# A one-layer streaming encoder step: spreading the last operand forms, a third sum of squares, an earlier root of x, and other loads in the head

## The chip, the cores and the metric

The kernel runs on one core of a Trainium2 chip. The metric is device time in microseconds of one execution. A core has a matrix engine (TensorE, "PE" in the profile, with its weight loads as "PEld"), VectorE ("DVE"), ScalarE ("ACT"), GpSimd ("POOL") and SyncE ("SP", which issues DMAs). Each engine works off its own queue in order; what is behind a waiting instruction waits too. A change is judged against the median of three runs of the kernel before.

## The reference, cut to what matters

Two groups of tokens, 512 of a prompt and 32 of a running stream, are put side by side as T = 544 columns. All is fp32.

```python
x  += concat(rmsnorm(short_conv(...)), rmsnorm(fox_attention(...))) @ w_out   # one input projection w_in for both
x  += cross_attention(rmsnorm(x), mk, mv, w_xq, w_xo)                         # 256 memory tokens, 4 heads
x  += square(relu(rmsnorm(x) @ w_up)) @ w_down                                # hidden 4 * 2048
y   = rmsnorm(x)                                                              # g_final
rmsnorm(x, g) = x * rsqrt(mean(x * x) + 1e-6) * g
logf = log_sigmoid(rmsnorm(x) @ w_f + b_f)                                    # 8 forget gates, part of w_in
```

D_MODEL is 2048, the hidden size of the MLP 8192. The outputs are y, the new keys, values and gates, and the last rows of the convolution.

## The kernel before, in words

Features lie on the 128 partitions and tokens on the free axis, so x is sixteen tiles of 128 x 544. Each fp32 operand is split in a high part that TensorE takes at its fast rate and the rest: `split(hi, lo, src)` is one ScalarE instruction (`hi`, line 84) and one VectorE instruction (`lo = src - hi`, line 85). A product then takes three matmuls: hi*hi, hi*lo, lo*hi. Weights come by DMA from SyncE as `raw` tiles and are split to `whi` and `wlo` in the same way, four buffers each.

The big projections work in a two-by-two block scheme with seven products: `operands` builds, from four 128 x 272 quarters of an input pair, the combinations `ts` and splits them (`oph`, `opl`); `combine` and `dsum` build the sums of weight blocks (`sum`). Weight sums and splits are given a priority 40 steps ahead of their place. The program is a list of operations that a scheduler puts in order for each engine, by its model of when each is ready; buffers of a pool with N slots are handed out again only when all reads of the former content, a DMA's included, are done.

The stages, in order of time, with the places that the change touches:

- **Head** (to about 60 us). Eight steps j load x tiles j and j+8 (`xr`) and one 128 x 1024 weight tile `w_first[j]`, scale x by the gain (`vec`), build the operands and run 48 matmuls into four PSUM pairs `heads`. The squares of x are summed: for j = 0 directly into two tiles `acc_x`, else by a square `sq` on ScalarE and a DMA on GpSimd's queue that adds it to `acc_x`. Behind the loop ScalarE copies the four pairs out (line 410), in the order 2, 3, 0, 1.
- **Gate product** `emit_logf` (line 430): 80 narrow matmuls with the weights of the forget gates, into a PSUM tile that is one of the two used by `heads`. The root of x, `rstd(acc_x)`, is called in `begin`, which is run in the first output pair of the input projection, between its third and fourth product; `begin` also scales the first four tiles by the root `rb` and runs the first convolution.
- Input projection, convolution, attention, output projection, cross-attention (to about 960 us).
- **Cross-attention's output** (about 915 to 976 us): `xo_done(m)` adds each output tile to x, squares it and scales it by the gain for the MLP; the squares go to two tiles `acc_3` by accumulating DMAs (line 1103). With the last tiles the first pair of MLP-up begins; `rstd(acc_3)` is called in that pair.
- **MLP-up** (to about 1650 us): 32 outputs. After each, `forms` writes seven combinations of the result as split operands to DRAM (`fd`). For the last two this is done in parts during MLP-down.
- **MLP-down** (1650 to 2333 us): eight column groups c with eight output pairs p each, 84 matmuls a pair. Products accumulate in PSUM tiles X, Y and Z; copies of intermediate states (`e1`, `e2`, lines 1350 to 1360) go out by ScalarE before X or Y is written again. For c = 0 and p = 1 to 6 one of six parts of `forms_in_parts` follows a pair; four of these hold four `put`s each. A `put` splits a 128 x 272 tile into `fp` (a tag with three buffers) and stores it by a DMA on GpSimd's queue. These forms are read in the last group, c = 7.
- **End** (2333 us on): the last output pair is done for the first half of the tokens (a = 0) and then the second (a = 1). `last_rstd` makes the root of each half, `finish` multiplies eight output pairs by it, `store` writes them. All eight of the first half are finished by VectorE, four behind each of the two outputs of a = 1; of the second half three are finished by GpSimd.

```python
        def put(dst, x):
            f = npool.tile([128, T], F32R, tag="rstd", name="fp", bufs=3)
            split(two(f)[:, 0], two(f)[:, 1], x)
            pool.dma_start(dst, f)
```

Of the kernel before, what the change touches and what calls it, by code (L numbers as in the profile page):

```python
# [41 lines left out]
def hybrid_step(  # L42
# [156 lines left out]
    def operands(x, b11, ts, tags):  # L199
        hi, lo = two(b11)[:, 0], two(b11)[:, 1]  # L200
        split(hi, lo, x[:, 0])
# [160 lines left out]
    for j in range(8):  # L362
        xr = [headp.tile([128, T], F32, tag="xr", name="xr", bufs=5) for i in range(2)]
        if j == 0:
            hi, lo = weights(w_first[j])
        for i in range(2):
            sp.dma_start(xr[i], xT[j + 8 * i])
        if j:
            hi, lo = weights(w_first[j])
        x = headp.tile([128, 4, TH], F32, tag="x", name="x", bufs=2)  # L370
        for i in range(2):
            if j + i == 0:
                dve.tensor_scalar(x[:, :2], two(xr[i]), gain(G_MIX, 0), None, ALU.mult)
            else:
# [13 lines left out]
        for i in range(2):  # L388
            if j:
                sq = tmp("sq")[:, :T]  # L390
                act.activation(sq, xr[i], AF.Square)
                pool.dma_start(acc_x[i], sq, accum_op=ALU.add)
            else:
                act.activation(acc_x[i], xr[i], AF.Square)
# [13 lines left out]
    for t, ps in ((2, heads[2]), (3, heads[3]), (0, heads[0]), (1, heads[1])):  # L408
        for a in range(2):
            act.activation(two(first_tiles[t])[:, a], ps[a], AF.Copy)  # L410
# [13 lines left out]
    def emit_logf():  # L424
        ps = mm_tile()
        plan = (("b11", 0), ("b21", 8)), (("b11", 0), ("t1", 0), ("b22", 8))
        for a in range(2):
            seq = [(j + k0, o[name][n]) for name, k0 in plan[a] for j, o in enumerate(xops) for n in range(2)]
            for i, (k, x) in enumerate(seq):
                pe.matmul(ps[:16, a, :TH], wf_hl[:, k], x, start=i == 0, stop=i == len(seq) - 1)  # L430
        return ps
# [144 lines left out]
    def begin():  # L576
        rstd(acc_x, D, out=rb)
# [515 lines left out]
    def xo_done(m, ps):  # L1093
# [4 lines left out]
        if j == 0:  # L1098
            act.activation(acc_3[i], x, AF.Square)
        else:  # L1100
            sq = (tmp("sq") if j > 4 else up.tile([128, 1024], F32, tag="raw2", name="sq", bufs=4))[:, :T]
            act.activation(sq, x, AF.Square)
            pool.dma_start(acc_3[i], sq, accum_op=ALU.add)
# [3 lines left out]
        if i:  # L1107
            b11 = upform.tile([128, T], F32R, tag="b11", name="b11")
            ops.append(operands(xgs.pop(j), b11, up.tile([128, 2 * T], F32, tag="sum", name="ts"), "ABC"))
# [68 lines left out]
    def forms_in_parts(i, h1, h2):  # L1178
# [15 lines left out]
        def first():  # L1194
            put(fd[i][0], a[:, 0])
            put(bd[i - NF + 4], a[:, 1])
            put(fd[i][5], b[:, 0])
            put(fd[i][3], b[:, 1])

        def second():  # L1200
            for t, q in zip(box["t"], ((1, 2), (4, 6))):
                for n in range(2):
                    put(fd[i][q[n]], t[:, n])

        return [differences, first, second]
# [123 lines left out]
    for c in range(NF // 4):  # L1329
# [8 lines left out]
        for p in range(8 if c < NF // 4 - 1 else 7):  # L1338
# [21 lines left out]
            act.activation(e2[:, 1], X, AF.Copy)  # L1360
# [8 lines left out]
            if c == 0 and 1 <= p <= len(parts):  # L1369
                parts[p - 1]()  # L1370
# [8 lines left out]
    sums = []  # L1379
    for a in range(2):  # L1380
        y = fin[a, 7] = slot("AB"[a], F32, "yout")
        sums.append([t[:, TH * a:TH * a + TH] for t in acc_4])
        for i in range(2):
# [13 lines left out]
            if a:  # L1397
                if i == 0:
                    rb_4 = last_rstd(sums[0])
# [3 lines left out]
    rb_5 = tmp("rb")[:, :TH]  # L1403
    act.activation(rb_5, rb_4, AF.Copy)
# [86 lines left out]
```

## Time and profile before

| what | value |
| --- | --- |
| median of 3 runs | 2365.38 us (2365.28 to 2366.73) |
| profiled execution, its own time | 2366.75 us |
| its span, first to last instruction | 2364.9 us |
| mean granted TensorE clock | 0.994 |
| instructions | 47573, of them 18083 matmuls |
| TensorE, VectorE, ScalarE, GpSimd busy | 98%, 85%, 56%, 10% |

In a row of a group of instructions stand line, engine, operation, the tile written and those read, the number, then busy time, the mean duration in ns, and the idle time of the engine just before them with what ended it. In a row of the timeline stand start, duration, engine, line, operation, tiles, shape, and in brackets the engine's idle time before it and the releaser. In a row of waits stand who waited for whom, then the total in us, the times and the longest. A line number can be that of a helper: 84 and 85 are all splits.

### The profile page before, as it was taken

The page shows a single profiled execution, that of the slowest core. Times are in us where ns is not written, and L with a number is a line of the kernel's source. Part 1 is how long each engine was busy: PE and PEld are TensorE (multiplying, and loading weights), DVE is VectorE, ACT ScalarE, POOL GpSimd, SP SyncE. Part 2 cuts the span into 40 slices and gives each one's busy share as a digit, 9 for nine tenths or more (in the row PEclk, how much of TensorE's full clock was granted, in tenths as well). Part 3 has the DMA queues.
Part 4 walks back from the last instruction along what each step waited for, and adds up shares of the span by engine and source line. Part 5 has one row for each costly group of instructions (what it writes and reads, how often), then busy time and mean ns, then how long its engine had stood idle before and what let it go on. Part 6 is the DMA issues. An engine that isn't in the chain of part 4 may idle for free. (4 is left out here: it accounts for less than half of the span.)

```text
span 2364.9 us, 47573 instructions
## 1 busy us (share of the span) xinstructions
PE 2310.9 (98%) x18083; PEld 2281.7 (96%) x18083; DVE 2008.1 (85%) x3562; ACT 1317.8 (56%) x2569; POOL 246.8 (10%) x447
## 2 busy tenths in 40 slices
PE   8999999999999999899999999999899999999997
PEld 8899999999999998899999999999799999999997
DVE  7899988877767757999999999998788888888885
ACT  8454555555644546665566656665455555555564
POOL 2000011113200001111111111111000000000001
PEclk9999999999999999999999999999999999999998
DMA  9333345578434537655666556668773564565454
GB/s 249 117 105 129 109 159 167 164 233 306 145 93 153 161 104 221 204 192 190 203 191 203 182 188 202 192 196 290 272 252 129 206 240 159 171 234 208 128 174 123
DMA packets 169638, 434.31 MB, mean 184 GB/s; under 512 B 19960, under 2 KB 24752, under 8 KB 169408
## 3 DMA queue, kind: packets, MB, share of 16 engines
q1 hardware_dynamic: 111616, 315.90, 39.8%
q0 software_dynamic: 52288, 106.45, 15.4%
q10 hardware_dynamic: 5504, 8.93, 1.1%
q8 instruction: 141, 2.31, 0.4%
q14 instruction: 89, 0.73, 0.1%
HBM read 322.27 MB, written 97.78 MB: 178 GB/s over the span
## 5 line engine op out<-in xcount | busy, mean ns | idle before, releaser
L84 ACT ACTIVATE whi<-raw 128x512 fp32r<-128x512 f32 x661 | 416.5, 631 | 466.8 <-PE mmx L269 95.4
L84 ACT ACTIVATE whi<-sum 128x512 fp32r<-128x512 f32 x676 | 422.4, 630 | 416.5 <-PE mmx L269 186.2
L85 DVE TENSOR_TENSOR wlo<-raw,whi 128x512 fp32r<-128x512 f32 x661 | 453.4, 688 | 123.5 <-ACT whi L84 115.8
L85 DVE TENSOR_TENSOR wlo<-sum,whi 128x512 fp32r<-128x512 f32 x676 | 453.1, 686 | 88.1 <-ACT whi L84 85.3
L1276 PE MATMUL dx<-f,whi 128*128 128x272 f32 x2016 | 389.6, 289 | 14.3 <-ACT e L1350 7.9
L269 PE MATMUL mmx<-oph,wlo 128*128 128x272 f32 x1296 | 374.9, 289 | 2.6 <-DVE wlo L85 2.6
L269 PE MATMUL mmx<-oph,whi 128*128 128x272 f32 x1296 | 373.5, 288 | 1.3 <-ACT h L278 0.9
L269 PE MATMUL mmx<-opl,whi 128*128 128x272 f32 x1296 | 372.1, 287 | 0.0
L1276 PEld LDWEIGHTS dx<-f,whi 128*128 128x128 f32 x2016 | 317.6, 189 | 16.5 <-ACT e L1350 9.7
L1276 PE MATMUL mm<-f,whi 128*128 128x272 f32 x1512 | 292.1, 288 | 0.0
L1276 PE MATMUL dx<-f,wlo 128*128 128x272 f32 x1008 | 291.3, 289 | 0.0
L269 PE MATMUL mmy<-oph,whi 128*128 128x272 f32 x864 | 249.8, 289 | 6.3 <-ACT whi L84 5.1
L269 PE MATMUL mmy<-oph,wlo 128*128 128x272 f32 x864 | 249.1, 289 | 0.9 <-DVE wlo L85 0.9
L269 PE MATMUL mmy<-opl,whi 128*128 128x272 f32 x864 | 248.8, 288 | 0.0
L269 PEld LDWEIGHTS mmx<-oph,wlo 128*128 128x128 f32 x1296 | 244.0, 188 | 3.2 <-DVE wlo L85 3.2
L269 PEld LDWEIGHTS mmx<-oph,whi 128*128 128x128 f32 x1296 | 244.7, 189 | 1.9 <-ACT h L278 1.1
L269 PEld LDWEIGHTS mmx<-opl,whi 128*128 128x128 f32 x1296 | 244.2, 188 | 0.0
L1276 PEld LDWEIGHTS mm<-f,whi 128*128 128x128 f32 x1512 | 238.2, 189 | 0.0
L1276 PE MATMUL mm<-f,wlo 128*128 128x272 f32 x756 | 218.1, 289 | 0.0
L1276 PEld LDWEIGHTS dx<-f,wlo 128*128 128x128 f32 x1008 | 190.6, 189 | 0.0
L269 PEld LDWEIGHTS mmy<-oph,whi 128*128 128x128 f32 x864 | 162.9, 189 | 7.5 <-ACT whi L84 5.5
L269 PE MATMUL mmx<-b,whi 128*128 128x272 f32 x864 | 167.8, 291 | 1.3 <-DVE x2r L1095 1.1
(412 smaller groups left out, 4941.5 us busy)
## 6 DMA issues: line engine op xcount, KB each, us to landing
raw<-in_w_up SPq DMA_DIRECT2D x128, 512.0 KB, 3.8
raw<-in_w_dn SPq DMA_DIRECT2D x128, 512.0 KB, 4.6
f<-fd SPq DMA_DIRECT2D x224, 272.0 KB, 5.7
fd<-form POOLq DMA_DIRECT2D x180, 272.0 KB, 4.0
raw<-in_w_in SPq DMA_DIRECT2D x88, 512.0 KB, 3.9
raw<-in_w_out SPq DMA_DIRECT2D x32, 512.0 KB, 3.9
acc<-sq POOLq DMA_DIRECT2D x40, 272.0 KB, 4.9
kq<-hl POOLq DMA_DIRECT2D x32, 256.0 KB, 3.1
```

What stands on the lines that cost most here:

```text
L84: act.activation(hi, src, AF.Copy)
L85: dve.tensor_tensor(lo, src, hi.bitcast(F32), ALU.subtract)
L269: pe.matmul(ps, a[:, c], x, start=first and j == 0 and n == 0, stop=j == 7 and n == 2, skip_group_check=not first)
L1276: pe.matmul(ps, a[:, c], f[:, x], start=first and j == 0 and n == 0, stop=j == 3 and n == 2, skip_group_check=not first)
```

## The change

- Head: x of step j+1 is loaded behind the weights of step j, and the squares of step j+1 are made at the end of step j. In the first step the order of the loads is x tile 0, half of the weights, x tile 8, the other half; the second x tile is scaled, and the second weight half split, behind the split of `b11` (which is taken out of `operands` and stands before each call of it).
- The PSUM pairs of the head are copied out in the order 0, 2, 3, 1, one half by ScalarE and one by VectorE.
- `rstd(acc_x)` is called inside the gate product, behind its first 32 matmuls.
- From the eleventh output tile on, the squares of cross-attention's output go to a third tile, the first directly and five by VectorE additions; the root then sums three tiles.
- `forms_in_parts` returns nine steps for each of the two outputs in place of three, and one step follows each output pair from the second on. What a step issues on ScalarE is ordered behind that pair's copy of X at line 1360 (`issue_after` is an order in ScalarE's queue, not a semaphore).
- The output y has the layout (half, pair, partition, 544), so that a store is one row a partition.
- Of the first half's eight outputs VectorE finishes two and GpSimd three when the root is there, and VectorE the last three behind the loop.

```diff
+    raws = [wpool.tile([128, 1024], F32, tag="raw", name="raw", bufs=3)[:, :512] for i in range(2)]
+    xn = load_x(0, lambda i: sp.dma_start(raws[i], w_first[0, :, 512 * i:512 * i + 512]))
     for j in range(8):
+        xr = xn
         if j:
             hi, lo = weights(w_first[j])
+        else:
+            hi, lo = halves(raws[0], 512)
+        if j < 7:
+            xn = load_x(j + 1)
...
+        split(two(b11)[:, 0], two(b11)[:, 1], x[:, 0])
+        if j == 0:
+            act.activation(x[:, 2:], two(xr[1]), AF.Identity, scale=gain(G_MIX, 8))
+            more = halves(raws[1], 512)
+            hi, lo = Parts([hi, more[0]]), Parts([lo, more[1]])
...
+        if j == 0:
+            square_x(0, xr)
+        if j < 7:
+            square_x(j + 1, xn)
...
-    for t, ps in ((2, heads[2]), (3, heads[3]), (0, heads[0]), (1, heads[1])):
-        for a in range(2):
-            act.activation(two(first_tiles[t])[:, a], ps[a], AF.Copy)
+    for t in (0, 2, 3, 1):
+        act.activation(two(first_tiles[t])[:, 0], heads[t][0], AF.Copy)
+        dve.tensor_copy(two(first_tiles[t])[:, 1], heads[t][1])
...
+            if a == 0:
+                rstd(acc_x, D, out=rb)
...
     def begin():
-        rstd(acc_x, D, out=rb)
...
+        elif i == 0 and j == 5:
+            acc_3.append(npool.tile([128, T], F32, tag="rstd", name="acc", bufs=3))
+            act.activation(acc_3[2], x, AF.Square)
         else:
...
-            pool.dma_start(acc_3[i], sq, accum_op=ALU.add)
+            if j < 5:
+                pool.dma_start(acc_3[i], sq, accum_op=ALU.add)
+            else:
+                dve.tensor_tensor(acc_3[2], acc_3[2], sq, ALU.add)
...
-        return [differences, first, second]
+        steps = [differences]
+        for dst, x in ((fd[i][0], a[:, 0]), (bd[i - NF + 4], a[:, 1]), (fd[i][5], b[:, 0]), (fd[i][3], b[:, 1])):
+            steps.append(lambda dst=dst, x=x: put(dst, x))
+        for n, q in enumerate(((1, 2), (4, 6))):
+            for k in range(2):
+                steps.append(lambda n=n, k=k, q=q: put(fd[i][q[k]], box["t"][n][:, k]))
+        return steps
...
-        d = slice(TH * a, TH * a + TH)
-        (sp if p % 2 else act).dma_start(o_y[2 * p:2 * p + 2, :, d].rearrange("m p t -> p m t"), two(y))
+        (sp if p % 2 else act).dma_start(o_y[a, p], y)
...
-            act.activation(e2[:, 1], X, AF.Copy)
+            mark = act.activation(e2[:, 1], X, AF.Copy)
...
-            if c == 0 and 1 <= p <= len(parts):
-                parts[p - 1]()
+            if parts and c + p:
+                with tc.issue_after(mark.ins):
+                    parts.pop(0)()
...
-                for p in range(4 * i, 4 * i + 4):
+            if a and i == 0:
+                rb_4 = last_rstd(sums[0])
+                rb_5 = pooled(rb_4)
+                for p in (0, 1):
                     store(p, 0, finish((0, p), rb_4, dve))
+                for p in (2, 3, 4):
+                    store(p, 0, finish((0, p), rb_5, pool))
+    for p in (5, 6, 7):
+        store(p, 0, finish((0, p), rb_4, dve))
```

More of the change, by code (lines that the diff above doesn't have):

```diff
@@ L361, in hybrid_step, with load_x, square_x @@
     xops = []
-    for j in range(8):
+    def load_x(j, between=lambda i: None):
         xr = [headp.tile([128, T], F32, tag="xr", name="xr", bufs=5) for i in range(2)]
-        if j == 0:
-            hi, lo = weights(w_first[j])
         for i in range(2):
             sp.dma_start(xr[i], xT[j + 8 * i])
+            between(i)
+        return xr
+    def square_x(j, xr):
+        for i in range(2):
+            if j:
+                sq = tmp("sq")[:, :T]
+                act.activation(sq, xr[i], AF.Square)
+                pool.dma_start(acc_x[i], sq, accum_op=ALU.add)
+            else:
+                act.activation(acc_x[i], xr[i], AF.Square)
+    raws = [wpool.tile([128, 1024], F32, tag="raw", name="raw", bufs=3)[:, :512] for i in range(2)]
+    xn = load_x(0, lambda i: sp.dma_start(raws[i], w_first[0, :, 512 * i:512 * i + 512]))
+    for j in range(8):
+        xr = xn
         if j:
             hi, lo = weights(w_first[j])
+        else:
+            hi, lo = halves(raws[0], 512)
+        if j < 7:
+            xn = load_x(j + 1)
         x = headp.tile([128, 4, TH], F32, tag="x", name="x", bufs=2)
[L371 to L374, printed above, removed]
+        if j == 0:
+            dve.tensor_scalar(x[:, :2], two(xr[0]), gain(G_MIX, 0), None, ALU.mult)
+        else:
+            for i in range(2):
                 act.activation(x[:, 2 * i:2 * i + 2], two(xr[i]), AF.Identity, scale=gain(G_MIX, j + 8 * i))
@@ L387, in hybrid_step @@
                                   stop=j + i == 8 and n == 2)
[L388 to L394, printed above, removed]
+        if j == 0:
+            square_x(0, xr)
+        if j < 7:
+            square_x(j + 1, xn)
     wf_hl = tpool.tile([128, T + 4], F32R, tag="t", name="wf_hl")[:, :256].rearrange("p (k c) -> p k c", k=KD)
@@ L1108, in xo_done @@
             b11 = upform.tile([128, T], F32R, tag="b11", name="b11")
+            split(two(b11)[:, 0], two(b11)[:, 1], xgs[j][:, 0])
             ops.append(operands(xgs.pop(j), b11, up.tile([128, 2 * T], F32, tag="sum", name="ts"), "ABC"))
@@ L1192, in differences @@
             dve.tensor_tensor(t34[:, 1], b[:, 0], t12[:, 1], ALU.subtract)
[L1194 to L1203, printed above, removed]
-        return [differences, first, second]
+        steps = [differences]
[5 more added lines that the diff above has]
+        return steps
     rb_3 = []
@@ L1379, in hybrid_step, with pooled @@
     sums = []
+    def pooled(r):
+        rp = npool.tile([128, T], F32, tag="rstd", name="rp", bufs=3)[:, :TH]
+        act.activation(rp, r, AF.Copy)
+        return rp
     for a in range(2):
@@ L1396, in hybrid_step @@
             act.activation(two(y)[:, i], xa, AF.Identity, scale=gain(G_FIN, 14 + i))
[L1397 to L1400 removed]
+            if a and i == 0:
+                rb_4 = last_rstd(sums[0])
+                rb_5 = pooled(rb_4)
+                for p in (0, 1):
                     store(p, 0, finish((0, p), rb_4, dve))
+                for p in (2, 3, 4):
+                    store(p, 0, finish((0, p), rb_5, pool))
+    for p in (5, 6, 7):
+        store(p, 0, finish((0, p), rb_4, dve))
     rb_4 = last_rstd(sums[1])
[L1403 to L1404 removed]
+    rb_5 = pooled(rb_4)
     for p in range(8):
```

6 lines of the change are left out of this document (3 added, 3 removed).

## The prediction

> **What bounds the kernel now.** I read the page first, then the busy time by stage, then what TensorE waited for, then for each long wait the instructions of the engine that ended it.
>
> ```profile
> span 2364.9 us, 47573 instructions
> PE 2310.9 (98%) x18083; PEld 2281.7 (96%) x18083; DVE 2008.1 (85%) x3562; ACT 1317.8 (56%) x2569; POOL 246.8 (10%) x447
> ```
> ```profile
> 8.24:60.50 52.26, 51.21 (x384) 50.90 (x384) 43.38 (x90) 46.14 (x91) 12.25 (x14) 1.00 0.96 252
> 60.50:102.00 41.50, 38.28 (x284) 35.15 (x284) 33.02 (x64) 16.04 (x31) 1.11 (x2) 0.96 0.28 93
> 102.00:900.00 798.00, 797.21 (x6180) 779.78 (x6180) 638.30 (x1228) 410.90 (x821) 84.00 (x157) 1.00 0.49 158
> 900.00:980.00 80.00, 71.17 (x519) 67.00 (x518) 64.55 (x112) 54.66 (x101) 13.19 (x16) 0.96 0.79 226
> 980.00:1650.00 670.00, 668.19 (x5323) 667.53 (x5322) 622.56 (x1016) 407.52 (x759) 112.74 (x214) 1.00 0.62 199
> 1650.00:1730.00 80.00, 66.50 (x498) 65.40 (x497) 62.90 (x119) 36.85 (x79) 7.43 (x14) 0.96 0.75 263
> 2352.40:2364.90 12.50, 0.00 (x0) 0.00 (x0) 4.49 (x9) 0.40 (x1) 3.92 (x3) 0.50 0.70 240
> ```
> The columns are TensorE, weight loads, VectorE, ScalarE, GpSimd, granted clock, DMA share, GB/s. TensorE carries the kernel: in 102 to 900 it is idle for 0.8 us of 798. An edit pays only where TensorE stands still or runs slowly, and those places are few:
>
> ```profile
> PE mm L386 <- ACT b L84: 8.2, 1, 8.2
> PE dx L1276 <- ACT e L1350: 7.9, 8, 3.3
> PE dx L1276 <- ACT e L1360: 6.4, 2, 4.4
> PE mmy L269 <- ACT whi L84: 5.1, 2, 3.1
> PE mmx L269 <- DVE wlo L85: 2.6, 2, 2.3
> ...
> PE mmx L269 <- DVE x2r L1095: 1.1, 1, 1.1
> PE mm L430 <- ACT hr L410: 1.1, 1, 1.1
> PE mmx L269 <- ACT h L278: 0.9, 1, 0.9
> ```
> The start, the two `dx` rows (all but 0.7 us of them at 1650 to 1730), the seam into MLP-up (5.1 and 1.1), the seam behind the head (2.3 of the 2.6, and 0.9), and the head's evacuation (1.1). Behind the long ones the clock was halved too:
>
> ```profile
> 8.24:14.24 6.00, 6.00 (x26) 5.90 (x27) 5.95 (x20) 5.95 (x12) 0.00 (x0) 1.00 0.94 338
> ...
> 92.75:96.17 3.42, 3.29 (x14) 3.29 (x15) 3.42 (x9) 1.93 (x3) 1.11 (x2) 0.50 0.31 78
> ...
> 963.15:969.98 6.83, 4.75 (x19) 4.43 (x20) 5.82 (x12) 5.41 (x10) 1.38 (x2) 0.50 1.01 305
> 1662.88:1666.30 3.42, 3.38 (x15) 3.38 (x16) 3.42 (x8) 2.06 (x4) 0.53 (x1) 0.50 1.05 416
> 1686.78:1690.19 3.41, 3.41 (x17) 3.41 (x16) 3.41 (x7) 0.98 (x3) 0.00 (x0) 0.50 0.05 20
> ```
> A busy half-clock stretch of 3.4 us costs 1.7 us. The first row shows 26 matmuls in 6 us (0.23 us each, against 498 in 66.5, 0.13): the start runs at half rate as well, though no clock was recorded yet.
>
> **Late forms (`forms_in_parts`), the main term.** Before, 16 `put`s stand in six parts in the first pairs of MLP-down. In 1650 to 1730 TensorE and, behind its wait, ScalarE wait:
>
> ```profile
> PE dx L1276 <- ACT e L1350: 7.1, 3, 3.3
> ```
> ```profile
> ACT fp L84 <- DMA fd<-fp: 19.4, 7, 6.0
> ...
> ACT fp L84 <- DMA bd<-fp: 2.7, 1, 2.7
> ```
> `fp` has three buffers, each free only when its store has landed; ScalarE's queue is in order, so a `put` that waits for its buffer holds back `whi` and the copies `e` out of PSUM, and TensorE waits for `e`. The edit makes 18 steps, one per output pair of some 10.5 us, each ScalarE part queued behind the pair's second `e2` copy. Three buffers then turn over in 31 us, so the 22.1 us of ScalarE waits should vanish, and with them 7.1 + 6.4 = 13.5 us of TensorE idle in this stretch and 2 x 1.7 of half clock: 16.9. What is late next is VectorE:
>
> ```profile
> 1730.00:1817.80 87.80, 87.80 (x703) 87.80 (x702) 78.05 (x136) 46.21 (x92) 0.00 (x0) 1.00 0.54 189
> ```
> 89% busy, 9.3 us of a 10.5 us pair. A `put` adds one 128x272 operation (0.43, row at 2349.10 below): 9.8, still room. The two `differences` steps add four: 11.1 us, 0.6 over in one pair each. Bounds of that: nothing, if the sums and weight halves prepared ahead absorb it, and 1.2. I charge 0.5. ScalarE (53% here) and GpSimd's queue hide the rest; the h tiles keep four of the seven `tmp` buffers for longer, and the three that are left serve `e1` and `e2`, two a pair. **Gain 16.4.**
>
> **Third sum of squares.**
> ```profile
> 960.15 0.66 ACT L1102 ACTIVATE sq<-x2r 128x544 f32<-128x544 f32 x1 [3.36 <-issue]
> ```
> ```profile
> 951.94 0.88 POOL L1103 DMA_DIRECT2D acc<-sq  x1 [3.14 <-DMA acc<-sq]
> ```
> ```profile
> DMA to landing us min/median/max: 3.6/5.6/8.1
> ```
> ```profile
> 961.48 0.73 DVE L205 TENSOR_TENSOR ts<-x 128x544 f32<-128x544 f32 x1 [3.13 <-ACT x L1106]
> ```
> ScalarE stands 3.36 us with no named releaser: 951.94 plus the longest landing, 8.1, is 960.0, so I read it as a square waiting for a `tmp` buffer that an accumulating DMA still reads. `x` queued behind it holds VectorE for 3.13, VectorE's sum holds `whi`, and TensorE idles 3.1. The edit takes six squares off the DMA chain and gives VectorE five 128x544 adds (0.65 each, from four in 2.62 below: 3.3). Three fall ahead of that sum, so the sum comes 3.1 - 2.0 = 1.1 earlier; the halved clock behind it (19 matmuls in 4.75, so 2.4 lost) probably goes, but VectorE sets the pace there and I take half: **gain 2.3**. Ends: -0.2 (adds fully exposed), and all 6.6 of idle plus 2.4, or 9.0. I stay near the low end because VectorE is the engine that TensorE waits for here. The two extra sum matmuls at the root cost about 0.5, in the same stretch and inside the bounds.
>
> **Head.** Before, the whole 512 KB weight is issued ahead of x, and on both engines the weight halves come ahead of x:
> ```profile
> 4.99 1.15 ACT L84 ACTIVATE whi<-raw 128x512 fp32r<-128x512 f32 x2 [2.53 <-DMA raw<-in_w_first]
> ```
> ```profile
> 6.87 0.50 DVE L373 TENSOR_SCALAR x<-xr,vec 128x544 f32<-128x544 f32 x1
> ```
> ```profile
> vec<-in_vecs ACTq DMA_DIRECT2D x1, 60.5 KB, 4.4
> ```
> The gains `vec`, issued at 0.74, land at 5.1; with x first, VectorE's multiply ends at 5.64 and two 128x272 splits on ScalarE (0.4 each) give a first matmul at 6.45 against 8.24: gain 1.8 (0 if the loads only swap places, 2.6 if the multiply alone remained). The half-rate stretch may shorten; by the 3.4 us and 6.8 us lengths above it is somewhere between 3.4 and 6.8 long against 6.0 now, worth -0.4 to 1.3, and I take the middle, 0.4. Moving each next x and its squares forward adds no instruction; it lets the accumulation chain end earlier. Evacuating the first PSUM pair first, half on VectorE (idle there, next row), removes the 1.1 wait. **Gain 3.3.**
>
> **Root inside the gate product.** VectorE's rows:
> ```profile
> 62.11 1.22 DVE L230 TENSOR_TENSOR sum<-raw,raw 128x1024 f32<-128x1024 f32 x1 [7.53 <-DMA raw<-in_w_in]
> ```
> ```profile
> 72.62 0.69 DVE L85 TENSOR_TENSOR wlo<-sum,whi 128x512 fp32r<-128x512 f32 x1 [4.55 <-ACT whi L84]
> ```
> It idles 4.55 us before 72.62, then is so loaded with the root and the first convolution that TensorE waits 2.3 at 90.6 and 0.9 at 101. The root's eight 128x272 operations (8 x 0.43 = 3.4) and what hangs on `rb` can start some ten us earlier and fill that hole. Its eight ssq matmuls are only moved. Gain 2.3 + 0.9 + 1.7 of clock = **4.9**; the low end is 1, if only the root moves and the convolution stays.
>
> [...]
>
> **Tail.**
> ```profile
> 2346.57 2.62 DVE L1293 TENSOR_TENSOR yout<-yout,r 128x544 f32<-128x544 f32 x4
> 2349.10 0.43 DVE L1392 TENSOR_TENSOR x<-x,mm 128x272 f32<-128x272 f32 x1
> 2349.45 2.61 DVE L1293 TENSOR_TENSOR yout<-yout,r 128x544 f32<-128x544 f32 x4
> ```
> The last add (L1392) stands behind four finished outputs, the last root behind four more. Two go instead of four ahead of it (1.3 saved), three instead of four ahead of the root (0.5): 1.8. The last stores run 6.8 us on full DMA engines:
> ```profile
> 2356.50:2363.30 6.80, 0.00 (x0) 0.00 (x0) 0.93 (x2) 0.00 (x0) 1.65 (x2) 0.50 0.96 329
> ```
> Each output's rows are twice as long in the new layout (2176 bytes in place of 1088). That saves nothing at worst, and 1.4 us if the 329 GB/s of this row become the 416 of the row at 1662.88; I take 0.8, a little over the middle, because the queues are full here. **Gain 2.6.**
>
> **Sum.** 16.4 + 2.3 + 3.3 + 4.9 + 2.6 = 29.5 us. The profiled execution took 2366.75, so 2337.25; the median of the three runs stands 1.4 lower, which gives 2335.9. I say 2336. About 0.2% (4.7 us) is what a measurement of this kernel can tell from no change.
>
> **Rivals.** *VectorE becomes the bound of the 18 pairs* (chance 0.18): 9.8 of 10.5 us leaves 0.7, and an in-order wait of VectorE for the delayed ScalarE half can eat it; at 0.5 us a pair 9 come back: 2345. *The edges do not spread the `put`s*, two fall together and the buffer waits remain (0.06): only 13.1 is gained, 2352. *Only the late forms work*, the seams stay because VectorE is short there (0.06): 2349.
> *Slower* (0.06): a `put`'s second half sits on VectorE's queue ahead of the next weight half and waits until ScalarE's copy behind the sixth product; then every pair stalls as the `e` L1350 waits did, 7.1 in three, 2.4 each, 18 x 2.4 = 43: 2379. It ends slower from 1.9 us a pair on. Against it: VectorE already waits for that copy in every pair (`xb += e2`) and those pairs show no gap. *No change* within 0.2% (0.02) needs several of these in part.
> A small one inside the forecast (0.1): three finished outputs on GpSimd, 1.32 us each, hold VectorE's root; two operations held gives 2.6 back, 2339.
> ```profile
> L1293 POOL TENSOR_TENSOR yout<-yout,rb x3: 1322/1322/1332, 2354.2 to 2356.8; 128x544 f32<-128x544 f32 x3
> ```
> [...]
>
> **Chances and range.** The forecast holds 0.62 and has its own range of 2329 to 2342: 7 us down if start, MLP-up seam and tail come halfway to their upper ends, 6 up if they and the root come halfway to their lower ones. With the VectorE rival (2345) and the one at 2349 the range of 2328 to 2350 leaves out the rest, less than 2 in 10. Faster: 0.62 + 0.18 + 0.06 + 0.06 = 0.92, less 0.01 for overlap; same 0.03; slower 0.06.
>
> **What will show it.** Late forms: no ScalarE wait `fp` <- DMA, no `dx` <- `e` wait over 1 us, clock 1.00 behind 1650. Squares: no 3 us ScalarE hole before `sq`, `acc<-sq` issues in that stage down from 14 to 8. Head: first matmul near 6.5, no wait at the gate product. Root: no waits between 85 and 102. Tail: last add two outputs earlier. A wait `dx` <- VectorE `wlo` in the first 18 pairs would prove me wrong in the main term.

## The result, and the profile after

| kernel | median | runs | ratio to before, 95% interval |
| --- | --- | --- | --- |
| before | 2366.06 us | 2365.28 to 2367.22 (4) | |
| changed | 2343.54 us | 2342.26 to 2345.03 (4) | 0.9905 [0.9887, 0.9922] |

The change takes 22.5 us off, where 29.5 were forecast; the measured time lies 7.5 us above the forecast 2336. The direction was right, and so was the outer range of 2328 to 2350. But the forecast's own range, 2329 to 2342, was missed by 1.5 us: the time fell to where the prediction had put two rivals, 2345 and 2349, and neither of them is what happened. That the outer range held is in part luck. In the profiled executions the spans are 2364.9 and 2342.9 us.

The opening of the page of the changed kernel, to set against that of before:

```profile
span 2342.9 us, 47597 instructions
PE 2307.8 (99%) x18087; PEld 2277.5 (97%) x18087; DVE 2010.9 (86%) x3568; ACT 1317.4 (56%) x2566; POOL 245.9 (10%) x444
```
TensorE still carries the kernel. It is busy 3.1 us less; the stretches at half clock between the head and the tail held 14.8 us of matmuls before and hold 6.3 now. Where the time went is read by stage. The table gives start times, from the traces, of single TensorE instructions that end each stage; a gain is the difference of two stages.

| TensorE instruction | before | changed | gained up to here | in this stage | forecast |
| --- | --- | --- | --- | --- | --- |
| first matmul of the gate product (head) | 60.52 | 57.81 | 2.70 | 2.70 | 3.3 |
| last `mmx` ahead of that tile's long pause, 545 to 966 before (root) | 545.02 | 537.92 | 7.10 | 4.40 | 4.9 |
| 101st `mmx` behind the pause, in MLP-up (third sum of squares) | 993.92 | 986.99 | 6.94 | -0.16 | 2.3 |
| first of MLP-down | 1649.30 | 1642.32 | 6.98 | 0.0 | 0 |
| last `mm` of MLP-down (late forms) | 2346.83 | 2322.89 | 23.94 | 16.96 | 16.4 |
| end of the span (tail) | 2364.95 | 2342.88 | 22.07 | -1.87 | 2.6 |

By these two traces two of the five terms failed, the third sum of squares and the tail. What TensorE waited for in the changed kernel, the longest rows and the largest that is left of the `dx` waits (waiter, what it waited for, us in total, times, longest):

```profile
PE mm L408 <- ACT b L84: 7.4, 2, 6.2
PE ssq L1321 <- ACT sq L1422: 3.5, 1, 3.5
PE mmy L268 <- ACT whi L84: 2.0, 2, 1.7
PE mmx L268 <- DVE wlo L85: 1.4, 3, 0.6
...
PE mmy L268 <- DVE opl L85: 1.2, 1, 1.2
PE dx L1298 <- ACT e L1371: 0.8, 5, 0.2
```
The `dx` waits of 7.9 and 6.4 us are down to five of at most 0.2, and the seam behind the head has no wait left. New is `ssq` <- `sq`, 3.5 us in the tail. The 5.1 us of `mmy` <- `whi` became 2.0, but `opl` and `wlo`, both VectorE's, came in their place.

Three stretches of the changed kernel (TensorE, weight loads, VectorE, ScalarE, GpSimd, granted clock, DMA share, GB/s):

```profile
968.39:975.22 6.83, 6.29 (x29) 6.12 (x28) 4.50 (x10) 1.65 (x4) 0.00 (x0) 0.50 0.44 154
1650.00:1730.00 80.00, 79.68 (x633) 79.23 (x633) 75.14 (x134) 44.33 (x90) 3.20 (x6) 1.00 0.74 262
1730.00:1817.80 87.80, 87.80 (x703) 87.80 (x702) 80.44 (x145) 48.60 (x99) 3.75 (x7) 1.00 0.67 224
```
In 1650 to 1730 TensorE did 498 matmuls before and does 633 now, at full clock. Of four stretches at half clock between the head and the tail one is left, at the seam into MLP-up, and it now lies on 6.29 us of work where it lay on 4.75.

### The profile page after: what moved, and what is told of

The parts are those of the page before. It is cut to its first block, busy times and chain, and to the rows that moved or that the text cites. A ratio compares the mean times of both kernels' runs of the same rounds, so it can differ in the third digit from the quotient of the medians.

```text
span 2342.9 us, 47597 instructions
## 1 busy us (share of the span) xinstructions
PE 2307.8 (99%) x18087; PEld 2277.5 (97%) x18087; DVE 2010.9 (86%) x3568; ACT 1317.4 (56%) x2566; POOL 245.9 (10%) x444
## 4 chain that ended last, share of the span: by engine, by line
PE 65%; issue 30%; DVE 2%; DMA 2%; POOL 1%; ACT 0%; POOLq 0%; SPq 0%; DVEq 0%; ACTq 0%
PE mmx L268 26%; PE mmy L268 13%; PE mm L120 12%; PE mmz L268 7%; PE mm L951 1%; PE h L408 1%; PE mm L408 1%; PE s L681 1%; DMA acc<-sq 1%; PE o L737 1%; DMA raw<-in_w_xo 1%; PE pt L715 0%; PE mm L449 0%; DVE wlo L85 0%; POOL fd L1212 0%
```

## The experiments

Each kernel ran beside the kernel before, whose median moved between 2366.1 and 2367.6 us; where less than 1.5 us matters, ratios or stages of the profile are compared. Starts of stages are taken at the instructions of the table above.

One pair of traces says less than its two decimals, since kernels with the same code in a stage do not take the same time in it. The gate product starts at 56.9 to 57.9 us in the ten kernels with the changed head, and at 59.6 and 60.5 in the two with the head of before. The stage with the seam into MLP-up takes 448.9 to 449.6 us in the seven kernels with the changed kernel's seam. The tail takes 18.6 to 20.0 us in the seven with the changed kernel's tail.

### Late forms: the steps, or the order on ScalarE?

Alone on the kernel before:

```diff
+        steps = [differences]
+        for dst, x in (...four...): steps.append(lambda dst=dst, x=x: put(dst, x))
+        ... four more single puts
-            if c == 0 and 1 <= p <= len(parts):
-                parts[p - 1]()
+            if parts and c + p:
+                with tc.issue_after(mark.ins):
+                    parts.pop(0)()
```


> The kernel before with the late forms alone (18 steps, one a pair, ScalarE part behind the pair's last e2 copy). Theory (the ScalarE waits for fp buffers in MLP-down are the whole gain of this part): 17.0 us less between the first product of MLP-down and its 20th pair, nothing anywhere else, span 2348 and time 2349 +- 1.5. Rival (the parts of the change feed each other, so that the forms alone give only part): span 2352 or more.

Measured 2350.22 us (2349.97 to 2351.47), ratio 0.9926 [0.9911, 0.994]. MLP-down to its last matmul was 17.2 us shorter than before. Its windows, in the same columns as above:

```profile
1650.00:1730.00 80.00, 79.96 (x636) 79.52 (x634) 74.50 (x134) 44.01 (x90) 2.68 (x5) 1.00 0.75 267
964.44:971.27 6.83, 6.24 (x27) 6.24 (x28) 5.75 (x11) 3.90 (x7) 1.73 (x2) 0.50 1.02 256
978.09:981.50 3.41, 2.95 (x13) 2.95 (x14) 2.39 (x5) 0.98 (x3) 0.00 (x0) 0.50 0.78 259
```
The first row is the whole term by itself. The two others show what takes some of it back in the total: at the seam into MLP-up, where this kernel's code is that of before, two stretches at half clock cover 9.2 us of matmuls, against 4.75 us in one before, and 2.3 us of the gain are given back there. A run of the same code at the same seam can thus differ by some 2 us by where the half clock falls. The span is 16.3 us shorter than before: 17.2, less these 2.3, and 1.0 in the head and 0.4 in the tail, which have the code of before as well.

Now the changed kernel with the steps but without the order on ScalarE's queue:

```diff
-                with tc.issue_after(mark.ins):
-                    parts.pop(0)()
+                parts.pop(0)()
```


> The changed kernel without the issue-order edges: still 18 steps in the program's text, one behind each pair, but nothing holds their ScalarE part back. Theory A (the edges matter: without them the forms are brought forward on ScalarE's queue, as far as buffers allow, and wait for fp buffers again): 10 us or more of ScalarE waits fp <- DMA in the first 80 us of MLP-down, time about 2355. Theory B (spreading the steps in the program is enough): waits under 1 us and the time of the changed kernel, 2343.5.

Measured 2357.8 us (2356.68 to 2358.04), ratio 0.9957 [0.994, 0.9973]: 14 us slower than the changed kernel. Its waits in MLP-down's first pairs, and two rows of ScalarE's timeline there (start, duration, then the idle time and its releaser in brackets):

```profile
ACT fp L84 <- DMA fd<-fp: 20.1, 8, 6.3
...
PE dx L1298 <- ACT e L1371: 5.7, 2, 3.6
PE dx L1298 <- ACT e L1381: 4.9, 2, 4.7
```
```profile
1653.57 0.43 ACT L84 ACTIVATE fp<-acc 128x272 fp32r<-128x272 f32 x1 [6.21 <-DMA fd<-fp]
...
1655.26 0.38 ACT L1381 ACTIVATE e<-dx 128x272 f32<-128x272 f32 x1
```
The pairs' steps are spread in the source, yet the scheduler puts the `fp` splits together as soon as its model has them ready. Each waits for one of three buffers, and a copy `e` stands behind. Most of the stall of before is back (22.1 us of ScalarE waits then, 20.3 now; 13.5 us of `dx` waits then, 10.6 now), with two stretches at half clock. MLP-down gains only 3.0 us. So the order on ScalarE's queue carries the term, and the split in 18 steps alone little of it.

### The tail: which queue holds the last square?

In the changed kernel's timeline, from the root of the first half on:

```profile
2323.20 3.94 POOL L1315 TENSOR_TENSOR yout<-yout,rp 128x544 f32<-128x544 f32 x3 [10.87 <-PE mm L1418]
...
2324.41 0.43 DVE L1420 TENSOR_TENSOR x<-x,mm 128x272 f32<-128x272 f32 x1
2324.57 2.93 ACTq L1334 DMA_DIRECT2D out_y<-yout  x3
...
2327.61 0.43 ACT L1422 ACTIVATE sq<-x 128x272 f32<-128x272 f32 x1 [4.50 <-POOL yout L1315]
...
2328.09 1.28 PE L1321 MATMUL ssq<-sq,inv 128*128 128x272 f32 x2 [3.54 <-ACT sq L1422]
```
The last add ends at 2324.84, two finished outputs earlier than before, as forecast. But its square starts at 2327.61, and the row says what ScalarE waited for: not the add but GpSimd's `yout`. Outputs 0, 2 and 4 are stored from ScalarE's queue (`ACTq`), and output 4 is the third that GpSimd finishes, at 2327.14. The square stands behind the issue of that store. Then the two matmuls come after a 3.5 us gap, at half clock (0.50 granted from 2328.0 to 2329.4).

This edit sends what GpSimd finishes in the first half to SyncE's queue:

```diff
-    def store(p, a, y):
-        (sp if p % 2 else act).dma_start(o_y[a, p], y)
+    def store(p, a, y, q=None):
+        (q or (sp if p % 2 else act)).dma_start(o_y[a, p], y)
...
-                    store(p, 0, finish((0, p), rb_5, pool))
+                    store(p, 0, finish((0, p), rb_5, pool), sp)
```


> The changed kernel; the three outputs of the first half that GpSimd finishes are stored by SyncE alone, where pair 2 and pair 4 were stored by ScalarE. Theory (in the changed kernel ScalarE's last square stands in its queue behind the store of pair 4, which waits for GpSimd's third output, 2.8 us): the square follows the last add within 0.1 us, TensorE's wait for it falls from 3.5 to about 0.8, span 3.0 to 3.5 us shorter, 2339.6. Rival (GpSimd's work slows VectorE's root through shared memory access, or the square waits for something else): the square still comes 2 us or more behind the add, span 2342 to 2343.

Measured 2340.28 us (2339.16 to 2340.9), ratio 0.9882 [0.9867, 0.9897]. From the last `mm` to the end it took 16.5 us, against 20.0 in the changed kernel and 18.1 before. The same rows in this kernel:

```profile
2323.80 0.43 ACT L1422 ACTIVATE sq<-x 128x272 f32<-128x272 f32 x1 [1.76 <-DVE x L1420]
```
```profile
2324.29 0.73 PE L1321 MATMUL ssq<-sq,inv 128*128 128x272 f32 x2 [0.80 <-ACT sq L1422]
```
The square now follows the add, and the sum follows the square, at 0.73 us in place of 1.28. Two DMA issues moved to another queue, those of outputs 2 and 4. Output 2 was done at 2324.54, ahead of the add's end, so it was output 4 that held the square. In these two traces 3.5 us come back: the square starts 2.0 us behind the last `mm` in place of 4.7, and the sum took another 0.55 less.

Six other kernels here have the changed kernel's tail. Their square starts 4.6 to 4.7 us behind the last `mm` as well, so the hold on the queue is the same. In five of them the sum took 0.72 to 0.73 us, and the tail 18.6 to 19.3; in the sixth it took 1.27, and the tail 19.8. The changed kernel's trace, with 1.28 at a granted clock of 0.50, shows the unlucky case.

The other half of the question: the tail with all of the old order of finishing (VectorE finishes the first half's eight) and the new layout of y:

```diff
-            if a and i == 0:
-                ... two finished by VectorE, three by GpSimd; three by VectorE behind the loop
+            if a:
+                if i == 0:
+                    rb_4 = last_rstd(sums[0])
+                for p in range(4 * i, 4 * i + 4):
+                    store(p, 0, finish((0, p), rb_4, dve))
```


> The changed kernel with the finishing order of the kernel before at the end (VectorE finishes all eight outputs of the first half, four behind each output pair; the new layout of y stays). It tells the layout's worth from the order's. Theory (the order lost 2.4 us, the layout gained 0.5): last product to end of span 17.6 against 18.1 in the kernel before and 20.0 in the changed one, span 2340.5. Rival (the layout cost time): 18.5 or more.

Measured 2341.76 us (2341.41 to 2342.59), ratio 0.9889 [0.9875, 0.9904]. From the last `mm` to the end 18.04 us, against 18.12 before and 17.74 in the kernel with the late forms alone, whose tail is that of before: the longer rows of a store show no gain, where 0.8 was forecast. Against this kernel the order of finishing as changed is a loss of 2.0 us in the changed kernel's trace, of 0.6 to 1.3 in the five others whose sum took 0.72 to 0.73 us, and with the stores moved a gain of 1.6. The two rows of this kernel show the delay in front of the last add, which has four finished outputs ahead of it:

```profile
2324.23 0.43 DVE L1420 TENSOR_TENSOR x<-x,mm 128x272 f32<-128x272 f32 x1
...
2324.69 0.43 ACT L1422 ACTIVATE sq<-x 128x272 f32<-128x272 f32 x1 [4.54 <-DVE x L1420]
```
The add ends 2.8 us behind the last `mm` (which started at 2321.88) here, and 2.0 us behind it in the changed kernel: 0.8 saved.

Is there a next wait in the mended tail? In it and in the changed kernel SyncE's queue ends with outputs of the second half, one of them finished by GpSimd. An edit on top of the mended tail lets GpSimd finish two of the last eight and not three:

```diff
-        store(p, 1, finish((1, p), rb_5 if p in (2, 4, 7) else rb_4, pool if p in (2, 4, 7) else dve))
+        store(p, 1, finish((1, p), rb_5 if p in (2, 4) else rb_4, pool if p in (2, 4) else dve))
```


> The changed kernel with two edits of its tail: the stores of the outputs that GpSimd finishes in the first half go to SyncE's queue (as in the run that gave 2340.3 us), and in the second half GpSimd finishes outputs 2 and 4 only, VectorE the other six, so that no output of GpSimd stands at the end of SyncE's queue. In the first of these runs the last matrix product ended 16.5 us before the end of the span, and the DMA engines were nearly full from 2325 to 2336 us with one dip to 249 GB/s near 2330. Theory A (after the queue is mended, the wait for GpSimd's third output is the next thing): the dip fills, 0.5 to 1.2 us less than that run, 2339.0 to 2339.8 us. Theory B (the 16 stores of 272 KB at the 350 to 410 GB/s seen are now the bound): no difference from it beyond 0.3 us, 2340 to 2340.6 us.

Measured 2340.49 us (2339.44 to 2341.01), ratio 0.9882 [0.9868, 0.9897]; last `mm` to end 16.46 us against 16.47. No difference. The 13 us of stores in the mended tail, then in this kernel, then 4 us of the changed kernel's, while its root is made:

```profile
2323.00:2336.00 13.00, 1.21 (x5) 0.35 (x3) 7.59 (x14) 2.16 (x5) 6.98 (x6) 0.72 0.91 343
```
```profile
2323.60:2336.60 13.00, 1.18 (x4) 0.32 (x3) 8.21 (x15) 2.16 (x5) 5.68 (x5) 0.61 0.92 343
```
```profile
2329.00:2333.00 4.00, 0.37 (x1) 0.00 (x0) 2.52 (x6) 1.31 (x3) 0.71 (x1) 0.50 0.58 218
```
Once the root is no longer late, the DMA engines are 91 to 92% busy at 343 GB/s in these 13 us, while in the changed kernel they are 58% busy as the root is made. The second of the two theories holds: GpSimd's third output was not the next thing. That the stores themselves now bound the tail fits the two rows, but no run changed their bytes or number.

### The third sum of squares: what did VectorE's adds cost?

The changed kernel with two sums by DMA, as before:

```diff
-        elif i == 0 and j == 5:
-            acc_3.append(...)
-            act.activation(acc_3[2], x, AF.Square)
...
-            if j < 5:
-                pool.dma_start(acc_3[i], sq, accum_op=ALU.add)
-            else:
-                dve.tensor_tensor(acc_3[2], acc_3[2], sq, ALU.add)
+            pool.dma_start(acc_3[i], sq, accum_op=ALU.add)
```


> The changed kernel with the squares of cross-attention's output as before (all by accumulating DMAs into two tiles). Theory A (the part took away ScalarE's 3.4 us hole, but its five VectorE additions cost as much, so it is worth nothing): the hole is back, VectorE has a 3 us hole too, and the time from the input projection's last product to the 100th product of MLP-up stays within 1 us of the changed kernel's 449.1; time 2343.5. Theory B (prediction: worth 2.3): 451.4 and 2345.8.

Measured 2344.26 us (2343.73 to 2344.82), ratio 0.9903 [0.9889, 0.9918], the time of the changed kernel. TensorE's waits at its seam, the longest of ScalarE's waits there, and then two views of the changed kernel:

```profile
PE mmy L268 <- ACT whi L84: 5.4, 2, 3.4
PE mmx L268 <- DVE x2r L1115: 1.4, 1, 1.4
```
```profile
ACT sq L1122 <- issue: 3.7, 1, 3.7
```
```profile
ACT sq L1125 <- DVE x2r L1115: 5.3, 7, 2.5
```
```profile
L1129 DVE TENSOR_TENSOR acc<-acc,sq 128x544 f32<-128x544 f32 x5 | 3.6, 720 | 0.4 <-ACT sq L1125 0.4
```
The first two fences are of the kernel without the third sum: a wait of TensorE of 3.4 us, near the 3.1 of before, is back, and with it the hole in which ScalarE waits for nothing that the profile names, 3.7 us. The third sum did take away both. The two others are of the changed kernel, ScalarE's waits from 930 to 972 and the adds on VectorE from 941 to 962 (busy time, mean ns, idle time ahead). Seven squares wait 5.3 us for VectorE's `x2r` there: VectorE stands still for 0.4 us in that stretch, and the five adds put 3.6 us of work into it. The stage from the last `mmx` ahead of the pause to the 101st behind it, in which the seam lies, takes 450.4 us without the third sum and 449.1 with it, against 448.9 before. In it TensorE waits 9.4 us without the third sum and 6.4 with it. About 0.9 of these 3.0 us go to the sums at the root: the trace has twelve rows `ssq<-acc` with three tiles and eight with two, and eight of them take 2.00 us.

So the edit is worth 1.4 us in this pair, and -0.2 against the trace of before. The three kernels with two tiles (before, the late forms alone, and this one) took 448.9, 451.2 and 450.4 us; the seven with three tiles from the eleventh output on took 448.9 to 449.6. The means differ by 1.1 us, which is less than the place of the half clock made in the kernel with the late forms alone.

If VectorE is short, GpSimd could add:

```diff
-                dve.tensor_tensor(acc_3[2], acc_3[2], sq, ALU.add)
+                pool.tensor_tensor(acc_3[2], acc_3[2], sq, ALU.add)
```


> The changed kernel with the five additions of squares on GpSimd (idle there, 1.3 us for such an operation at the end of the kernel) in place of VectorE. Theory A (VectorE's load is what TensorE waits for at this seam): TensorE's waits between 950 and 971 fall from 5.0 to 2 or less, no or a shorter half-clock stretch, 3 to 5 us less, 2339.5. Theory B (GpSimd and VectorE disturb each other at the memory): VectorE's operations beside GpSimd's become longer than their 0.72 us and the gain is lost, 2343. Theory C (the last square's sum comes later, GpSimd being slower, and the root with it): TensorE waits at the root's sums instead.

Measured 2346.02 us (2344.84 to 2347.77), ratio 0.9911 [0.9897, 0.9926]: no gain, and the stage takes 450.7 us in place of 449.1. Two of the five adds on GpSimd's timeline, then VectorE's operations beside them:

```profile
943.34 1.43 POOL L1129 TENSOR_TENSOR acc<-acc,sq 128x544 f32<-128x544 f32 x1 [4.92 <-ACT sq L1125]
...
951.34 1.86 POOL L1129 TENSOR_TENSOR acc<-acc,sq 128x544 f32<-128x544 f32 x1 [2.53 <-ACT sq L1125]
```
```profile
943.47 1.85 DVE L85 TENSOR_TENSOR wlo<-raw,whi 128x512 fp32r<-128x512 f32 x1
...
951.29 2.45 DVE L85 TENSOR_TENSOR wlo<-raw,whi 128x512 fp32r<-128x512 f32 x2
```
A `wlo` of 0.68 us takes 1.85 when it starts 0.13 us behind GpSimd's add, and ends 0.55 us after it (945.32 and 944.77). In the second place VectorE began first, its two `wlo` took 2.45, and GpSimd's add took 1.86 in place of 1.43. So an add moved off VectorE, 0.72 us there, costs it about 1.2 us (1.15 to 1.19 in four of the five, 0.7 in the last). The rows show the two engines holding each other up, whichever of them began; by what means was not shown. The prediction's small rival supposed such a hold in the tail, where no row of before shows it.

Fewer adds on VectorE then: the third sum begins one chunk later, with three adds, and the squares of chunk 5 go by DMA.

```diff
-        elif i == 0 and j == 5:
+        elif i == 0 and j == 6:
...
-            if j < 5:
+            if j < 6:
                 pool.dma_start(acc_3[i], sq, accum_op=ALU.add)
```


> The changed kernel, but the third tile of squares begins one chunk later (the first half's chunk 6 instead of 5), so that VectorE makes three adds instead of five and the squares of chunk 5 go by DMA again. Theory A (the adds took from VectorE about the time that the removed wait of ScalarE gave, five adds of 0.63 to 0.72 us = 3.4 us in a stretch in which VectorE has no gap): with 1.3 us less on VectorE the waits of TensorE at this seam fall from 5.0 us to 3.5 to 4.2 us and the kernel takes 0.8 to 1.3 us less, 2342.3 to 2342.8 us. Theory B (what is lost at this seam is lost to the stretch at half clock, which follows any gap): the waits fall but the half-clock stretch of 6.8 us stays, time within 0.5 us of 2343.5. Theory C (the DMA's accumulate of chunk 5 is late): the wait of ScalarE for the sum of squares is back, above 1 us, and the time is that of the kernel without the third tile, about 2344.3 us.

Measured 2342.4 us (2341.53 to 2343.0), ratio 0.9891 [0.9876, 0.9906]. The stage took 448.4 us in place of 449.1. TensorE's waits at the seam:

```profile
PE mmy L268 <- ACT whi L84: 1.7, 1, 1.7
PE mmy L268 <- ACT oph L84: 1.1, 1, 1.1
PE mmy L268 <- DVE opl L85: 0.9, 1, 0.9
...
PE mmx L268 <- DVE wlo L85: 0.3, 1, 0.3
```
4.0 us, where the changed kernel has 5.0, and the half-clock stretch of 6.83 us stays. The waits at the seam fell as the first theory had it, while those ahead of it, from 868 to 898 us, grew by 0.9, and ScalarE's wait for the sum by DMA did not return. A gain of 0.7 us by itself is less than the measurement can tell.

### Root of x

```diff
-            if a == 0:
-                rstd(acc_x, D, out=rb)
...
     def begin():
+        rstd(acc_x, D, out=rb)
```


> The changed kernel with the root of x called in begin again. Theory (the root inside the gate product lets VectorE work in its 4.6 us hole, worth 4.9 by the prediction, 4.4 by the two traces): waits of TensorE of 2 to 3 us between 85 and 102 come back, with a half-clock stretch behind them; first gate product to the projection's last product 484.5 as in the kernel before against 480.1; time 2347.9. Rival (it is the earlier squares and the split evacuation that opened the hole): 481 or less, time 2344.

Measured 2348.01 us (2347.05 to 2351.85), ratio 0.9922 [0.9907, 0.9937]; 4.5 us behind the changed kernel, all of it gone by the end of the projection's stage. TensorE's waits between 60 and 110 us, and a window:

```profile
PE mmx L268 <- DVE wlo L85: 2.3, 1, 2.3
PE mmx L268 <- ACT h L277: 0.9, 1, 0.9
```
```profile
90.64:94.05 3.41, 3.41 (x17) 3.41 (x17) 3.41 (x8) 1.93 (x3) 1.11 (x2) 0.50 0.47 119
```
VectorE's timeline of this kernel, then that of the changed one:

```profile
69.92 0.69 DVE L85 TENSOR_TENSOR wlo<-sum,whi 128x512 fp32r<-128x512 f32 x1 [3.96 <-ACT whi L84]
```
```profile
67.48 0.43 DVE L184 TENSOR_TENSOR rb<-rb,nt 128x272 f32<-128x272 f32 x1
...
68.63 0.72 DVE L599 TENSOR_TENSOR hr<-hr,rb 128x544 f32<-128x544 f32 x1
```
With the root back in `begin` the hole of 4 us on VectorE, both waits and the half clock behind them are there again. In the changed kernel root and first scalings fill the hole. 2.3 + 0.9 + 1.7 = 4.9 was the sum; 4.4 to 4.5 is the measurement.

The half clock, however, was no part of the price. The kernel with the late forms alone has the code of before in this stage. The 7 us behind the gap, in the kernel before and then in that one (TensorE, weight loads, VectorE, ScalarE, GpSimd, granted clock, DMA share, GB/s):

```profile
93.00:100.00 7.00, 7.00 (x45) 7.00 (x46) 7.00 (x19) 3.19 (x5) 1.11 (x2) 0.77 0.53 156
```
```profile
92.00:99.00 7.00, 6.18 (x46) 5.78 (x47) 7.00 (x19) 3.08 (x5) 1.11 (x2) 1.00 0.53 156
```
Its gap of 2.27 us was followed by full clock, and its stage from the gate product on still took 484.5 us, as before. VectorE is busy without a break in both rows. With a faster clock TensorE only waits for VectorE again, 1.0 us more in three short gaps. What the edit took away is VectorE's lateness.

### Order of loads in the head

The changed kernel with the head's loop of before, its evacuation order kept:

```diff
-    raws = [...]                      # half weights, x ahead of them, squares one step early
-    xn = load_x(0, ...)
...
+    for j in range(8):
+        xr = [headp...]               # as before
```


> The changed kernel with the head's loads, order of squares and first step as before; the evacuation and the root as in the changed one. Theory (the load order is worth 2.0 at the first product and some 1 to 1.5 by the shorter half-rate start): first product 8.2, first gate product at 59.5 against 57.8, time 2345.5. Rival (later steps of the head take the gain back, as the 1.2 us wait at 13.6 says): first gate product under 58.5 all the same, time 2344.

Measured 2344.75 us (2343.05 to 2344.97), ratio 0.9903 [0.9887, 0.992]. The first matmul starts at 8.16 (6.22 in the changed kernel), the gate product at 58.90 (57.81). Of 1.94 us gained at the start only 1.09 are left at the end of the head in this pair; over the ten kernels with the changed head it is 1.0 to 2.0. The changed kernel's TensorE in the second step, and ScalarE ahead of it:

```profile
15.08 0.76 PE L408 MATMUL mm<-b,whi 128*128 128x272 f32 x4 [1.17 <-ACT b L84]
```
```profile
9.08 0.64 ACT L372 ACTIVATE sq<-xr 128x544 f32<-128x544 f32 x1
...
10.18 0.64 ACT L372 ACTIVATE sq<-xr 128x544 f32<-128x544 f32 x1
11.40 0.66 ACT L84 ACTIVATE oph<-ts 128x544 fp32r<-128x544 f32 x1 [0.58 <-DVE ts L208]
...
14.29 0.73 ACT L84 ACTIVATE b<-x 128x272 fp32r<-128x272 f32 x2
```
TensorE waits 1.17 us for that step's split `b` (and 0.18 for VectorE's half); the kernel with the old order has no such wait. Two squares of the next step, moved forward, stand ahead of the split on ScalarE's queue with 1.2 us. They are not shown to be its cause: behind them ScalarE stands idle for 0.58 us, until VectorE's `ts` is done, so in this order they delay nothing that comes later.

Nor does the wait cost anything that the end of the head shows. The ten kernels differ in how long half rate held at the start, up to the first granted clock on record. Where it held for 3.0 to 3.2 us (three kernels), TensorE waited 0.6 to 1.2 us for `b`; where it held for 4.9 to 6.1 (the other seven), no wait was longer than 0.2. From the first matmul to the gate product the three took 51.0 to 51.6 us and the seven 50.9 to 51.7. A shorter half rate shows no gain here. The other 1.6 us of the head's 2.7, which the kernel with the old order keeps, are the evacuation's 1.1 and 0.5 that were not traced.

### Both mends together

The mended tail (both edits) and the later third sum:

> Both edits together: the mended tail and the later third tile. If they act in different places their differences add: the tail's 3.3 to 4.5 us less than the changed kernel and what the later third tile gives by itself; 2338.2 to 2340 us. A sum that falls short by more than 1 us would say that one of them is disturbance of the clock at the seam and not work.

Measured 2338.3 us (2337.62 to 2338.58), ratio 0.9873 [0.9856, 0.9889], the fastest of all: 5.2 us below the changed kernel by the medians, 6.1 by the profiled spans. From the last `mm` to the end it takes 16.7 us, the tail's 3.3 us again. The stage with the seam takes 447.3 us, 1.8 less than in the changed kernel. Its stretch at half clock:

```profile
964.72:971.55 6.83, 5.21 (x22) 4.57 (x22) 5.83 (x9) 2.76 (x6) 0.00 (x0) 0.50 0.46 154
```
5.21 us of matmuls lie in it, in place of 6.29, and half of the difference is time. So 0.5 of the 1.8 us is the half clock's place; TensorE's waits in the stage sum to 5.4 us against 6.4, which is another 1.0; the remaining 0.2 was not traced. The two edits add, with a share of chance in the half clock.

## Why the prediction was right and wrong, by its own steps

**Late forms** (forecast 16.4, measured 17.0, and 17.2 alone). Right in mechanism and size. ScalarE has no `fp` <- DMA wait, TensorE no `dx` wait over 0.2 us, and the clock is 1.00 behind 1650. The 0.5 us charged for VectorE was not spent: VectorE goes from 89 to 92% of a pair's time and TensorE does not stand still for it. The rival with VectorE as the bound of the 18 pairs (2345) fell with that, though the time came near its number for another reason. The rival that the edges would not spread the `put`s is what the kernel without them shows.

**Third sum of squares** (2.3, measured -0.2 against before, 1.4 when undone). Two steps failed. The first is the half of the clock's loss that was added as gain (1.2): the stretch of 6.83 us stays, with 1.5 us more of matmuls in it, which at the granted 0.50 costs 0.8. The second is "two extra sum matmuls at the root cost about 0.5": they are four rows in the trace, some 0.9 us. The wait on the DMA chain did go, and the accumulating DMAs in the stage fell from 14 to 8, but in a stretch where VectorE has no gap five adds delay all that hangs on it, ScalarE's squares too (5.3 us of waits for `x2r`). TensorE's waits at the seam fell from 6.6 us to 5.0, or from 7.2 in the kernel without the third sum. That is 1.6 to 2.2 us; less the longer sums 0.7 to 1.3 are left, where "1.1 earlier" was forecast. Against before the waits at 894 to 905 us, ahead of the seam, fell by another 0.8, and some 0.9 of the stage was not traced. So the low end, -0.2, "adds fully exposed", came as a number, but by another sum.

**Head** (3.3, measured 2.7). First matmul at 6.22 (6.45 forecast), and the 1.1 us wait at the gate product is gone. Against the trace of before the ten kernels with this head give 2.6 to 3.6, so the size was right. The 0.4 for a shorter half rate was not: half rate held for 3.0 to 6.1 us with the same code, in three kernels for less than the 3.4 named as its least, and the head did not end sooner there. The kernel with the late forms alone, with the head of before, was 1.0 us faster through it, so 0.6 us between forecast and measurement says nothing. "Moving each next x and its squares forward adds no instruction" is true, but it changes the order on ScalarE's queue, and the forecast did not ask what that does.

**Root inside the gate product** (4.9, measured 4.4, and 4.5 undone). Right in that the hole on VectorE was the room. The size was in part luck: 1.7 of it was half clock, and the kernel with the late forms alone shows that this stage takes 484.5 us without the half clock as well, since VectorE sets the pace. That the half clock adds its full 1.7 to the price was the author's estimate; without it the sum is 3.2. The measured 4.4 does not decide between 4.9 and 3.2: what is missing from the 3.2 is more waiting for VectorE, not the clock.

**Tail** (2.6, measured -1.9; -0.5 to -1.2 in the five kernels whose sum took 0.72 to 0.73 us). The step that failed is the 1.8: "Two go instead of four ahead of it (1.3 saved), three instead of four ahead of the root (0.5)". VectorE's order came as forecast, though the add gained 0.8 and not 1.3, since the finishing now waits 0.47 us for ScalarE's copy of the root. But the prediction looked at the queue of the engine that computes and not at ScalarE's, on which a store that waits for GpSimd stands ahead of the last square. It is the rule that the prediction applied to the `put`s, not applied to the stores. With the stores of GpSimd's outputs on SyncE's queue the tail gains 1.6. The layout's 0.8 did not come: 18.04 us with the long rows, 18.12 and 17.74 with the short ones. The small rival, GpSimd holding VectorE's root, did not occur: VectorE's finishing operations took 0.65 us apiece beside GpSimd's (1.97 for three, 3.24 for five), as in the kernel before (2.62 for four). Such a hold was seen with the adds on GpSimd, at the seam, about 1.2 us at a time.

## What to carry to other kernels

An instruction that issues a DMA held its engine's queue here: the store of output 4, waiting for GpSimd, kept the last square 2.8 us behind its add. So for each store, ask which engine makes its data and what stands behind it, and put stores of a slow engine's output on a queue with nothing behind them. An order in the source is no order on an engine when a scheduler sits between; where pace matters, as with three buffers and sixteen stores, tie each step to an instruction of that engine (without the tie the kernel took 14 us more). Work is moved to an engine only at a place where that engine has a gap: the root found a hole of 4 us and brought nearly all that was forecast, the squares found none, and of 2.3 us at most 1.4 came. And a stretch at half clock is not a loss by itself: at the seam into MLP-up more of it cost 2.3 us, while behind the head, where VectorE set the pace, the stage took the same time without it.

## What the runs showed of the hardware

- No gap of TensorE in 950 to 975 was longer than 1.7 us in the changed kernel, and half clock came at 968.39 all the same, behind gaps of 0.7, 1.2 and 1.7 us in the 5 us ahead of it. Behind the head a gap of 2.28 us was followed by half clock in two kernels (before, and the root back in `begin`), and one of 2.27 at the same matmul was not in a third (the late forms alone). So the length of a single gap did not tell what the clock would do.
- The stretches at half clock between the head and the tail that the windows of nine kernels give were 3.41 to 3.42 or 6.83 us long. The one at the seam into MLP-up began at 966.84 in the kernel with the later third sum and at 964.72 in the one with both mends, which has the same code up to there. Why its place moves was not shown, and what the seam would take without the half clock stays open.
- With the adds on GpSimd, GpSimd and VectorE held each other up: 1.2 us added to a `wlo` of 0.68 us, and 0.4 us to GpSimd's 1.43.
- A store's rows of 2176 bytes in place of 1088 made no difference that these traces show in the tail: 18.04 us against 18.12 and 17.74.
